# Stick-breaking attention in a hybrid trunk: weights summed by parts, with differences of neighbouring values

## The chip, the core and the metric

The kernel runs on one core of one Trainium2 chip. The metric is the device time of the whole program in microseconds (us). The core's engines are TensorE (PE; its weight loads are shown apart as PEld), VectorE (DVE), ScalarE (ACT), GpSimd (POOL) and SyncE (SP, which here issues nearly all DMAs). Each works through its own instructions in the order in which they were built, and waits at an instruction until what it needs is there.

## What is computed

The input is one sequence of 2048 tokens with 1024 features, float32. An even layer normalizes it, projects it to queries, keys and values of 8 heads of 128, to a gate, and to the input of a state-space mixer with a gate of its own, joins both branches and projects back; an odd layer is gated linear attention. The part that matters here is the attention of the even layer:

```python
z = jnp.einsum('bthd,bshd->bhts', qf[:, q0:kend], kf[:, :kend])
...
causal = s_idx < t_idx
log_beta = jax.nn.log_sigmoid(z)
log_one_minus = jnp.where(causal, log_beta - z, 0.0)
rest = lax.cumsum(log_one_minus, axis=3, reverse=True) - log_one_minus
w = jnp.where(causal, jnp.exp(log_beta + rest), 0.0)
outs.append(jnp.einsum('bhts,bshd->bthd', w, vf[:, :kend]))
```

A query t gives the key s the weight beta(t,s) times the product of 1 - beta(t,j) over all keys j between s and t. Its output is the sum of the weighted values.

Write p(t,s) for the product of 1 - beta(t,j) over all j from s to t - 1. Then beta(t,s) times the product behind it is p(t,s+1) - p(t,s), so the sum over keys can be written by parts: the value of the last key of the block, plus the sum over s of p(t,s) times (value of s - 1 less value of s), with zero for the value ahead of the first token.

## The kernel before, in words

Every matmul operand is split into a high and a low part (`split`, L310: a copy on ACT makes the high part, a subtraction on another engine the low one), and three products of the parts stand for one (`mm3`, L66). The program runs in stages: the gates' projections and the state-space branch first (to about 598 us of the profiled execution), then attention (598 to 1752 us), then the output projection and the odd layer.

`attention` (L668) loops over 8 heads; in a head over 4 macro tiles m of 512 tokens; in a macro tile over 4 token tiles of 128. For a token tile, ACT and POOL split the normalized input (`sh` L711, `sl` L712), PE makes query, key and value together in 24 matmuls of 384 columns (`pp`, L67 to L69), ACT squares the query and key and sums them (`qk` L719), POOL makes the two reciprocal roots (`qkms` L54, `qkrs` L56), DVE scales (`qn` L725), PE transposes (`tp` L728). The value is taken from PSUM by ACT (`vhi` L721) and DVE (`vlo` L722).

Then come two pairs of query blocks for the macro tile, each against the key chunks c = m, m - 1, ..., 0 of 512 keys. For each of the pair's two blocks: PE makes the scores (`z`), ACT takes sigmoid(-z) into `om` (L760) and sigmoid(z) into `be` (L762), DVE runs the product from the last key to the first (`pt`, L764, a scan that begins with the value that the chunk to the right left), POOL multiplies `be` by it (L768), PE transposes the result (`w`, L771), ACT and DVE split that (`th` L773, `tl` L774). With both blocks done PE multiplies by the values (`av`, L782), DVE applies the gate (`ot`, L785), and SP stores it (L786) and loads the next gate (`zs`, L739).

The order on each engine is made by the scheduler of the tile framework, which is asked to place instructions by its own timing model; by it the projections of a macro tile lie among the attention work of the one before, and the next head's weights (L660) are loaded toward the end of a head. There are two buffers for `sh` and `sl`, two PSUM banks for `z`, two for `w`, and three buffers for `be` and for `pt`.

Of the kernel before, what the change touches and what calls it, by code (L numbers as in the profile page):

```python
# [9 lines left out]
F32 = mybir.dt.float32  # L10
# [3 lines left out]
ALU = mybir.AluOpType  # L14
# [35 lines left out]
def rsqrt_mean(e, pool, ss, n, dim, tag):  # L50
    """1 / sqrt(ss / dim + EPS) for a [P, n] tile of sums of squares."""
# [8 lines left out]
def behind(e, i, first):  # L60
    """i comes behind first in their engine's queue"""
    e.tc.add_manual_dep(i.ins, first.ins.name, mybir.DependencyInfo(
        mybir.DependencyClass.NoSync, mybir.DependencyReason.DATA), reason="order")
# [8 lines left out]
class Norm:  # L72
    """hT[m][p, k, t] = rms_norm(x)[m * 512 + t, k * 128 + p], a token tile at a time"""
# [48 lines left out]
def s5_angles(e, s, lam_re, lam_im, log_dt):  # L122
    """lam, dt and sines of the angle of lam_bar and of its half; partitions and columns as in s5_setup"""
# [32 lines left out]
def s5_setup(e, room, lr, li, dt, sn, sh, b_re, b_im, c_re, c_im, dsk, bin_d, k0_d, co_d):  # L156
    """Chunk matrices of the SSM (8 tokens a chunk) into DRAM, powers of lam_bar into e.pw.

    Partition q = (parity, n) of pair i holds state n of group 2 * i + parity.
    bin_d[ri, i, (j, p), q] = lam_bar^(7-j) b_bar;  co_d[ri, i, q, (t, p)] = c lam_bar^(t+1)  # L160
    k0_d[g, (j, pi), (t, po)] = Re(c lam_bar^(t-j) b_bar) + d [t == j, pi == po]
    """
# [3 lines left out]
    # lam_bar^8, ^16, ^32, ^64: real parts, and (-im, im)  # L166
    e.pwr = [e.cst.tile([P, NI], F32, name=f"pwr{a}") for a in range(4)]
    e.pwi = [e.cst.tile([P, 2, NI], F32, name=f"pwi{a}") for a in range(4)]
    with e.pool("s5s", 1, "right") as s, e.pool("s5t", 2, "right") as s2, e.pool("s5w", 1, "right") as sw, \
# [41 lines left out]
        # powers  # L211
# [13 lines left out]
        def cmul(outs, xr, xi, yr, yi, sub, E):  # L225
            """outs[0] = xr yr + sub * xi yi, outs[1] = xr yi - sub * xi yr, x small, broadcast"""
# [24 lines left out]
        # G[tau] = c lam_bar^tau: real part, and minus the imaginary part  # L251
# [23 lines left out]
        # four groups at a time, on the partitions from 0, 32, 64 and 96  # L275
# [22 lines left out]
        # onto 16 partitions, then each row block of the chunk matrix  # L298
# [13 lines left out]
def split(nc, hi, lo, src, lo_eng):  # L312
    """hi + lo == src, each of 12 significant bits"""
# [7 lines left out]
# order in which a panel's last macro tile takes the weights: from low addresses on  # L321
# [3 lines left out]
class Panels:  # L325
    """Pools for weight panels of up to 512 columns, and for splits of hT."""
# [45 lines left out]
# token tiles to norm after these products (half, column block, row block)  # L372
# [3 lines left out]
def first_gates(e, pn, nrm, hT, w, c0, out_d, setup):  # L376
    """The first macro tile of gates(), as its tokens and weights come; returns the weights, and setup()."""
# [42 lines left out]
def gates(e, pn, hT, w, c0, out_d, row0, lo_eng, between=None, also=None, ws=None, sp=None, last=LAST):  # L420
    """out_d[row0 + f, t] = silu(h w[:, c0 + f]) for 512 columns; between(m) is called before macro tile m
# [925 lines left out]
```

## Time and profile before

| what | us |
|---|---|
| median of 3 runs | 2915.71 |
| lowest and highest run | 2911.27 and 2917.75 |
| span of the profiled execution | 2920.8 |
| of it, attention | 1154 |

The span runs from the first to the last instruction of the profiled execution. No separate time of that execution is given beside its span; the three runs are other executions. A row of the profile names line, engine, operation and tiles as out<-in; "busy" is the time in which an engine's instructions ran, and the idle time before an instruction is put down to what came last of the things that it waited for. Matmuls overlap one another, so the length of one in a row is longer than the step from one to the next.

### The profile page before, as it was taken

The page shows a single profiled execution, that of the slowest core. Times are in us where ns is not written, and L with a number is a line of the kernel's source. Part 1 is how long each engine was busy: PE and PEld are TensorE (multiplying, and loading weights), DVE is VectorE, ACT ScalarE, POOL GpSimd, SP SyncE. Part 2 cuts the span into 40 slices and gives each one's busy share as a digit, 9 for nine tenths or more (in the row PEclk, how much of TensorE's full clock was granted, in tenths as well). Part 3 has the DMA queues.
Part 4 walks back from the last instruction along what each step waited for, and adds up shares of the span by engine and source line. Part 5 has one row for each costly group of instructions (what it writes and reads, how often), then busy time and mean ns, then how long its engine had stood idle before and what let it go on. Part 6 is the DMA issues. An engine that isn't in the chain of part 4 may idle for free.

```text
span 2920.8 us, 46867 instructions
## 1 busy us (share of the span) xinstructions
PE 2795.6 (96%) x17433; PEld 2508.1 (86%) x17433; DVE 1766.5 (60%) x2789; ACT 1476.4 (51%) x3244; POOL 1446.3 (50%) x1513
## 2 busy tenths in 40 slices
PE   7989979899999999999999989999999999999999
PEld 6788767898989898989898978888788999999887
DVE  7768965757686767676767674223344556565521
ACT  5475224556666656665656663222345556555310
POOL 7102821478787878787878752000023465555300
PEclk9999989999999999999999999999999999999999
DMA  5532136411010101010102114333131111121343
GB/s 167 153 79 79 58 103 216 142 30 33 19 33 19 33 19 33 22 34 19 33 19 65 48 44 141 105 104 93 58 101 37 37 59 55 41 73 62 115 142 112
DMA packets 217011, 207.17 MB, mean 71 GB/s; under 512 B 24528, under 2 KB 185712, under 8 KB 216272
## 3 DMA queue, kind: packets, MB, share of 16 engines
q1 hardware_dynamic: 216208, 202.08, 22.5%
q8 instruction: 138, 2.26, 0.3%
q10 hardware_dynamic: 576, 2.10, 0.2%
q14 instruction: 89, 0.73, 0.1%
HBM read 129.29 MB, written 74.58 MB: 70 GB/s over the span
## 4 chain that ended last, share of the span: by engine, by line
PE 73%; DVE 8%; POOL 8%; issue 5%; ACT 3%; DMA 3%; SPq 1%; POOLq 0%; ACTq 0%; DVEq 0%
PE av L782 5%; PE pp L68 5%; PE pp L67 5%; PE ops L68 5%; PE pp L69 5%; PE ops L67 5%; PE ops L69 5%; PE gps L67 4%; PE gps L68 3%; PE gps L69 3%; PE w L771 3%; DVE pt L764 2%; PE qk L67 2%; PE qk L69 2%; PE qk L68 2%
## 5 line engine op out<-in xcount | busy, mean ns | idle before, releaser
L768 POOL TENSOR_TENSOR be<-be,pt 128x512 f32<-128x512 f32 (+2 forms) x320 | 359.1, 1128 | 162.5 <-DVE pt L764 87.5
L712 POOL TENSOR_TENSOR sl<-hT,sh 128x1024 fp32r<-128x1024 f32 x128 | 331.6, 2591 | 65.0 <-ACT sh L711 64.0
L68 PE MATMUL pp<-wlo,sh 128*128 128x384 f32 x1024 | 353.0, 345 | 8.0 <-POOL wlo L315 8.0
L67 PE MATMUL pp<-whi,sh 128*128 128x384 f32 x1024 | 356.8, 349 | 2.3 <-ACT whi L314 2.3
L69 PE MATMUL pp<-whi,sl 128*128 128x384 f32 x1024 | 348.4, 340 | 0.0
L764 DVE TENSOR_TENSOR_SCAN pt<-om,pt,zero 128x513 f32<-128x513 f32 x192 | 318.7, 1660 | 19.6 <-ACT om L760 12.5
L67 PE MATMUL gps<-sh,whi 128*128 128x512 f32 (+1 forms) x672 | 253.2, 390 | 24.0 <-DVE sg L365 20.7
L68 PE MATMUL gps<-sl,whi 128*128 128x512 f32 (+1 forms) x672 | 259.3, 387 | 3.4 <-DVE sl L315 3.3
L69 PE MATMUL gps<-sh,wlo 128*128 128x512 f32 (+1 forms) x672 | 257.0, 385 | 0.0
L773 ACT ACTIVATE th<-w 128x512 fp32r<-128x512 f32 (+2 forms) x320 | 171.9, 542 | 114.1 <-PE w L771 113.0
L774 DVE TENSOR_TENSOR tl<-w,th 128x512 fp32r<-128x512 f32 (+2 forms) x320 | 187.3, 597 | 66.2 <-ACT th L773 64.7
L760 ACT ACTIVATE om<-z 128x512 f32<-128x512 f32 (+2 forms) x320 | 174.5, 545 | 104.2 <-PE z L69 75.5
L68 PEld LDWEIGHTS pp<-wlo,sh 128*128 128x128 f32 x1024 | 193.7, 189 | 18.1 <-POOL wlo L315 15.6
L315 DVE TENSOR_TENSOR sl<-hT,sh 128x1024 fp32r<-128x1024 f32 (+1 forms) x148 | 173.0, 1192 | 51.0 <-ACT sh L314 49.0
L67 PEld LDWEIGHTS pp<-whi,sh 128*128 128x128 f32 x1024 | 195.0, 190 | 8.2 <-ACT whi L314 5.4
L69 PE MATMUL ops<-woh,ol 128*128 128x512 f32 x496 | 196.7, 397 | 0.0
L68 PE MATMUL ops<-wol,oh 128*128 128x512 f32 x496 | 196.3, 396 | 0.0
L67 PE MATMUL ops<-woh,oh 128*128 128x512 f32 x496 | 195.6, 395 | 0.0
L69 PEld LDWEIGHTS pp<-whi,sl 128*128 128x128 f32 x1024 | 193.0, 189 | 2.4
L314 ACT ACTIVATE sh<-hT 128x1024 fp32r<-128x1024 f32 (+1 forms) x148 | 155.6, 1090 | 61.6 <-PE gps L69 32.6
L711 ACT ACTIVATE sh<-hT 128x1024 fp32r<-128x1024 f32 x128 | 135.9, 1062 | 97.7 <-PE pp L68 97.1
L771 PE MATMUL w<-ident,be 128*128 128x128 f32 x1088 | 170.7, 274 | 8.5 <-POOL be L768 5.8
(326 smaller groups left out, 8249.2 us busy)
## 6 DMA issues: line engine op xcount, KB each, us to landing
zs_d<-sg SPq DMA_DIRECT2D x80, 256.0 KB
o<-o_d SPq DMA_DIRECT2D x80, 256.0 KB
xt<-in_x_dram SPq DMA_DIRECT2D x28, 512.0 KB
r<-in_even_w_in_dram SPq DMA_DIRECT2D x64, 192.0 KB
zs<-zs_d SPq DMA_DIRECT2D x64, 128.0 KB
o_d<-ot SPq DMA_DIRECT2D x64, 128.0 KB
r<-in_odd_w_in_dram SPq DMA_DIRECT2D x64, 128.0 KB
zs<-zs_d SPq DMA_DIRECT2D x32, 256.0 KB
```

Source lines behind the costliest of these rows:

```text
L67: nc.tensor.matmul(out, lhsT=lhi, rhs=rhi, start=start, stop=False)
L68: nc.tensor.matmul(out, lhsT=lhi, rhs=rlo, start=False, stop=False)
L69: return nc.tensor.matmul(out, lhsT=llo, rhs=rhi, start=False, stop=stop)
L314: a = nc.scalar.activation(hi, src, AF.Copy)
L315: b = lo_eng.tensor_tensor(lo, src, hi.bitcast(F32), ALU.subtract)
L712: nc.gpsimd.tensor_tensor(sl, ht, sh.bitcast(F32), ALU.subtract)
L760: nc.scalar.activation(o[:, lo:512], z[:, :n], AF.Sigmoid, scale=-scale)
L764: nc.vector.tensor_tensor_scan(pt[:, lo:][:, ::-1], o[:, lo:][:, ::-1], zr.to_broadcast([P, n + 1]), 1.0 if prev[i] is None else prev[i], ...
L768: nc.gpsimd.tensor_tensor(be[:, :n], be[:, :n], pt[:, lo + 1:513], ALU.mult)
L771: nc.tensor.transpose(w[:, s, :], be[:, s * P:(s + 1) * P], e.ident)
L773: nc.scalar.activation(th[:, :ni, qs], w[:, :ni, :], AF.Copy)
L774: nc.vector.tensor_tensor(tl[:, :ni, qs], w[:, :ni, :], th[:, :ni, qs].bitcast(F32), ALU.subtract)
```

## The change

The beta of a key and its product with the scan are gone. What is transposed is the scan itself, `pt`, and the values are replaced by differences of neighbouring values. The value goes from PSUM into `vf` (ACT, float32). Differences are made for two token tiles at a time (a half): DMAs move `vf` down by one partition into `dv` (rows 0 to 111 by one DMA, rows 112 to 126 by another, and for the first partition the last row of the tile before, by one DMA in the second half and one or two in the first), POOL subtracts, ACT and POOL split. The last value of each block of 128 is brought onto columns through DRAM (`ve_d`, `ve`) and added when the gate is applied, which is now two instructions instead of one. In the first half of a macro tile POOL's subtraction is held behind the `sl` of the last token tile. `pt` has four buffers instead of three.

```diff
         kvp = pool("at_kv", 5)
-        wk = pool("at_wk", 3)
+        vp = pool("at_v", 2)
+        wk = pool("at_wk", 4)
...
+                vf = vp.tile([P, 4, P], F32, tag="vf", name="vf")
                 for half in range(2):
...
-                        nc.gpsimd.tensor_tensor(sl, ht, sh.bitcast(F32), ALU.subtract)
+                        a = nc.gpsimd.tensor_tensor(sl, ht, sh.bitcast(F32), ALU.subtract)
+                        if i == 3:
+                            behind(e, sub, a)
...
-                        nc.scalar.activation(vhi[:, i, :], ps[:, 2, :], AF.Copy)
-                        nc.vector.tensor_tensor(vlo[:, i, :], ps[:, 2, :], vhi[:, i, :].bitcast(F32), ALU.subtract)
+                        nc.scalar.activation(vf[:, i, :], ps[:, 2, :], AF.Copy)
...
+                    i = slice(half * 2, half * 2 + 2)
+                    dv = vp.tile([P, 2, P], F32, tag="dv", name="dv")
+                    nc.sync.dma_start(out=dv[1:113], in_=vf[0:112, i])
+                    nc.sync.dma_start(out=dv[113:P], in_=vf[112:P - 1, i])
+                    if half:
+                        nc.sync.dma_start(out=dv[0:1], in_=vf[P - 1:P, 1:3])
+                    else:
+                        if m == 0:
+                            nc.vector.memset(dv[0:1, 0], 0.0)
+                        else:
+                            nc.sync.dma_start(out=dv[0:1, 0], in_=vl[P - 1:P, 3])
+                        nc.sync.dma_start(out=dv[0:1, 1], in_=vf[P - 1:P, 0])
+                    sub = nc.gpsimd.tensor_tensor(dv, dv, vf[:, i], ALU.subtract)
+                    split(nc, vhi[:, i], vlo[:, i], dv, nc.gpsimd)
+                    vl = vf
...
+                ve = vp.tile([P, 4], F32, tag="ve", name="ve")
+                nc.sync.dma_start(out=ve_d[h:h + 1, m * 4:m * 4 + 4], in_=vf[P - 1:P])
+                nc.sync.dma_start(out=ve, in_=ve_d[h, m * 4:m * 4 + 4].rearrange("i d -> d i"))
...
                             nc.scalar.activation(o[:, lo:512], z[:, :n], AF.Sigmoid, scale=-scale)
-                            be = wk.tile([P, 512], F32, tag="be", name="be")
-                            nc.scalar.activation(be[:, :n], z[:, :n], AF.Sigmoid, scale=scale)
                             pt = wk.tile([P, 513], F32, tag="pt", name="pt")
...
-                            nc.gpsimd.tensor_tensor(be[:, :n], be[:, :n], pt[:, lo + 1:513], ALU.mult)
                             w = wps.tile([P, 4, P], F32, tag="w", name="w")
                             for s in range(ni):
-                                nc.tensor.transpose(w[:, s, :], be[:, s * P:(s + 1) * P], e.ident)
+                                nc.tensor.transpose(w[:, s, :], pt[:, lo + s * P:lo + (s + 1) * P], e.ident)
...
-                    nc.vector.tensor_tensor(ot, av, zs, ALU.mult)
+                    for i in range(2):
+                        qs, b = slice(i * P, (i + 1) * P), pr % 2 * 2 + i
+                        nc.vector.scalar_tensor_tensor(ot[:, qs], av[:, qs], ve[:, b:b + 1], zs[:, qs], ALU.add, ALU.mult)
```

The scheduler orders the engines anew. Three places follow, all in the fifth head where the projections of the third macro tile (`hT2`) begin; numbers behind the names are buffer numbers and differ between the two programs.

First POOL before, from the split of the third macro tile's first token tile to a product in its third:

```order
L712 TENSOR_TENSOR sl_13761<-hT2_89,sh_13760 128x1024 [waits PE_49,Activation_49]
L54 TENSOR_SCALAR qkms_13498<-ss_13495 128x2 [waits Activation_49]
L56 TENSOR_TENSOR qkrs_13500<-qkms_13498,mhalf_68 128x2 [waits Pool_49]
L712 TENSOR_TENSOR sl_13805<-hT2_89,sh_13804 128x1024 [waits PE_49,Activation_49]
L54 TENSOR_SCALAR qkms_13542<-ss_13539 128x2 [waits Activation_49]
L768 TENSOR_TENSOR be_13568<-be_13568,pt_13570 128x128 [waits DVE_49,Activation_49]
L768 TENSOR_TENSOR be_13583<-be_13583,pt_13585 128x256 [waits DVE_49,Activation_49]
L56 TENSOR_TENSOR qkrs_13544<-qkms_13542,mhalf_68 128x2 [waits Pool_49]
L768 TENSOR_TENSOR be_13606<-be_13606,pt_13608 128x512 [waits DVE_49,Activation_49]
L712 TENSOR_TENSOR sl_13854<-hT2_89,sh_13853 128x1024 [waits PE_49,Activation_49]
L768 TENSOR_TENSOR be_13623<-be_13623,pt_13625 128x512 [waits DVE_49,Activation_49]
```

POOL after, from the same split on to that of the third token tile; `dv_13359` and `vlo_13169` are the second half of macro tile two:

```order
L719 TENSOR_TENSOR sl_13556<-hT2_89,sh_13555 128x1024 [waits PE_49,Activation_49]
L54 TENSOR_SCALAR qkms_13306<-ss_13303 128x2 [waits Activation_49]
L56 TENSOR_TENSOR qkrs_13308<-qkms_13306,mhalf_68 128x2 [waits DVE_49,Pool_49]
L719 TENSOR_TENSOR sl_13599<-hT2_89,sh_13598 128x1024 [waits PE_49,Activation_49]
L54 TENSOR_SCALAR qkms_13349<-ss_13346 128x2 [waits Activation_49]
L56 TENSOR_TENSOR qkrs_13351<-qkms_13349,mhalf_68 128x2 [waits DVE_49,Pool_49]
L750 TENSOR_TENSOR dv_13359<-dv_13359,vf_13172 128x256 [waits DMAHW5_49,DMAHW6_49,DMAHW0_49,Activation_49]
L315 TENSOR_TENSOR vlo_13169<-dv_13359,vhi_13168 128x256 [waits Activation_49]
L719 TENSOR_TENSOR sl_13655<-hT2_89,sh_13654 128x1024 [waits PE_49,Activation_49]
```

The products with beta are gone, and a subtraction and a low part for each half have come in, which stand behind the two reciprocal roots and ahead of the split of a token tile two further on.

Then ACT before, from the squares of the last token tile of the second macro tile (`pp_13513`) on:

```order
L719 ACTIVATE qk_13538,ss_13539<-pp_13513 128x128
L721 ACTIVATE vhi_13367<-pp_13513 128x128
L760 ACTIVATE om2_5874<-z_13562 128x128 [waits PE_49]
L762 ACTIVATE be_13568<-z_13562 128x128
L760 ACTIVATE om0_5872<-z_13577 128x256 [waits PE_49]
L762 ACTIVATE be_13583<-z_13577 128x256 [waits Pool_49]
L760 ACTIVATE om1_5873<-z_13601 128x512 [waits PE_49]
L762 ACTIVATE be_13606<-z_13601 128x512 [waits Pool_49]
```

ACT after, from the same squares on (`pp_13320`); `vhi_13168<-dv_13359` is the copy of the differences:

```order
L728 ACTIVATE qk_13345,ss_13346<-pp_13320 128x128 [waits PE_49,Activation_49]
L728 ACTIVATE qk_13345,ss_13346<-pp_13320 128x128
L730 ACTIVATE vf_13172<-pp_13320 128x128
L788 ACTIVATE om2_5875<-z_13378 128x128 [waits PE_49]
L788 ACTIVATE om0_5873<-z_13390 128x256 [waits PE_49]
L314 ACTIVATE vhi_13168<-dv_13359 128x256 [waits DMAHW5_49,DMAHW6_49,DMAHW0_49,Pool_49]
L788 ACTIVATE om1_5874<-z_13411 128x512 [waits PE_49]
L798 ACTIVATE th_13376<-w_13386 128x128 [waits PE_49]
L788 ACTIVATE om2_5875<-z_13425 128x512 [waits DVE_49,PE_49]
```

The second sigmoid of each score tile is gone; the copy of the value has become one to `vf`, and two sigmoids behind it stands the copy that waits for the DMAs and for POOL.

At last SP before, with a store and a gate load in turn:

```order
L786 DMA o_d_80<-ot_13022 128x256 [waits DVE_49]
L739 DMA zs_13311<-zs_d_79 128x256 [waits DMAHW6_49,DMAHW2_49]
L786 DMA o_d_80<-ot_13307 128x256 [waits DMAHW3_49,DVE_49]
L739 DMA zs_13558<-zs_d_79 128x256 [waits DMAHW4_49,DMAHW0_49]
L786 DMA o_d_80<-ot_13362 128x256 [waits DMAHW5_49,DVE_49]
L739 DMA zs_13651<-zs_d_79 128x256 [waits DMAHW2_49]
```

SP after, from the DMAs of the same second half on:

```order
L743 DMA dv_13359<-vf_13172 1x16x16 [waits DMAHW5_49,Activation_49,Pool_49]
L740 DMA dv_13359<-vf_13172 112x256 [waits DMAHW6_49,Activation_49]
L813 DMA o_d_80<-ot_13162 128x256 [waits DMAHW7_49,DVE_49]
L741 DMA dv_13359<-vf_13172 15x256 [waits DMAHW0_49]
L760 DMA ve_d_5864<-vf_13172 1x512 [waits DMAHW1_49]
L767 DMA zs_13456<-zs_d_79 128x256 [waits DMAHW2_49]
L748 DMA dv_13641<-vf_13172 1x16x8 [waits DMAHW3_49,Pool_49]
L761 DMA ve_13370<-ve_d_5864 128x4x1 [waits DMAHW4_49,DMAHW1_49]
L749 DMA dv_13641<-vf_13553 1x16x8 [waits DMAHW5_49,Activation_49]
```

Where SP had two DMAs for a pair of blocks, the pieces of `dv`, the store of the last values (`ve_d`) and their load (`ve`) have come in between; the store of a pair (`ot_13162`) stands between the two pieces of `dv_13359`.

## Rows read from the trace of the kernel before

**Rows 1.** The page's head and first part.

```profile
span 2920.8 us, 46867 instructions
...
PE 2795.6 (96%) x17433; PEld 2508.1 (86%) x17433; DVE 1766.5 (60%) x2789; ACT 1476.4 (51%) x3244; POOL 1446.3 (50%) x1513
```

**Rows 2.** Windows: us; busy of PE, PEld, DVE, ACT, POOL (count); granted clock; DMA share; GB/s.

```profile
598.00:1752.00 1154.00, 1118.57 (x7180) 1040.67 (x7180) 817.23 (x1219) 724.64 (x1907) 913.37 (x761) 1.00 0.10 31
1690.00:1752.00 62.00, 53.99 (x332) 46.63 (x333) 50.28 (x65) 38.68 (x80) 31.71 (x30) 0.97 0.17 50
1126.99:1269.72 142.73, 140.09 (x907) 130.65 (x906) 99.09 (x153) 90.58 (x240) 116.33 (x97) 1.00 0.09 27
```

**Rows 3.** Waits of PE, 598 to 1752 us: total us, times, longest.

```profile
PE tp L728 <- DVE qn L725: 10.8, 12, 3.3
PE pp L68 <- POOL wlo L315: 8.0, 10, 1.1
PE w L771 <- POOL be L768: 5.8, 16, 1.0
PE w L771 <- DVE tl L774: 2.4, 3, 1.0
...
PE pp L67 <- ACT whi L314: 2.3, 5, 0.6
PE av L782 <- ACT be L762: 1.5, 1, 1.5
```

**Rows 4.** Waits of all engines, same stretch.

```profile
DVE qn L725 <- POOL qkrs L56: 163.2, 106, 3.5
...
POOL be L768 <- DVE pt L764: 87.5, 97, 3.4
```

**Rows 5.** The page's fifth part: the multiply by beta, all shapes.

```profile
L768 POOL TENSOR_TENSOR be<-be,pt 128x512 f32<-128x512 f32 (+2 forms) x320 | 359.1, 1128 | 162.5 <-DVE pt L764 87.5
```

**Rows 6.** Groups by line and shape, 598 to 1752 us.

```profile
L762 ACT ACTIVATE be<-z 128x512 f32<-128x512 f32 x224 | 136.7, 610 | 0.0
...
L721 ACT ACTIVATE vhi<-pp 128x128 fp32r<-128x128 f32 x125 | 36.7, 294 | 0.0
L722 DVE TENSOR_TENSOR vlo<-pp,vhi 128x128 fp32r<-128x128 f32 x125 | 35.4, 283 | 28.5 <-ACT vhi L721 28.3
...
L785 DVE TENSOR_TENSOR ot<-av,zs 128x256 f32<-128x256 f32 x64 | 26.5, 415 | 30.9 <-PE av L782 30.8
...
L731 ACT ACTIVATE khi<-tp 128x256 fp32r<-128x256 f32 x63 | 24.3, 386 | 67.1 <-DVE qlo L732 67.0
...
L768 POOL TENSOR_TENSOR be<-be,pt 128x256 f32<-128x256 f32 x32 | 21.3, 667 | 6.5 <-ACT vhi L721 5.2 <-DVE pt L764 1.1 <-issue 0.2
```

**Rows 7.** Source line of the scan: ns min/median/max, first and last start.

```profile
L764 DVE TENSOR_TENSOR_SCAN pt<-om,pt,zero x192: 1260/1538/3393, 628.5 to 1742.6; 128x513 f32<-128x513 f32 x192
```

**Rows 8.** Source line of the gate's load: SP's own time for one issue.

```profile
L739 SPq DMA_DIRECT2D zs<-zs_d x64: 332/424/782, 586.7 to 1718.5; - x64
```

**Rows 9.** The chain of waits, whole run: start us, us, what.

```profile
155.78 2.02 DMA ka<-kt
...
522.28 6.43 DMA yk<-y_d
...
984.38 2.40 DMA r<-in_even_w_in_dram
```

**Rows 10.** Timeline of PE: start us, us.

```profile
1186.01 0.33 PE L68 MATMUL pp<-wlo,sh 128*128 128x384 f32 x1
1186.18 0.33 PE L69 MATMUL pp<-whi,sl 128*128 128x384 f32 x1
...
1187.63 0.28 PE L782 MATMUL av<-th,vlo 128*128 128x256 f32 x1
1187.75 0.28 PE L782 MATMUL av<-th,vhi 128*128 128x256 f32 x1
```

More of the change, by code (lines that the diff above doesn't have):

```diff
@@ L665, in load, with attention @@
         return out
-def attention(e, hT, w_in, zsT, oT, ap, w0, after):
+def attention(e, hT, w_in, zsT, oT, ve_d, ap, w0, after):
     nc, tc = e.nc, e.tc
@@ L1277, in after_head @@
             ow.early, ow.again = 6, (4, 5, 2, 3)
-    attention(e, hT, w0, zs_d, o_d, ap, aw, after_head)
+    attention(e, hT, w0, zs_d, o_d, dram("ve_d", [HEADS, NT, DH]), ap, aw, after_head)
     ow.pool("left")
```

## The prediction

> **What bounds the kernel now.** I read the page's head first, then windows, PE's waits, the waits of the other engines, and at last single rows for durations. PE is busy 96% of the span of 2920.8 us [rows 1]; no other engine is above 60%. The change touches attention alone, 598 to 1752 us. There PE is busy for 1118.57 of 1154 us at a granted clock of 1.00, so PE stands idle for 35.4 us, 3% of the stage [rows 2]. The work on PE is the same after the change: as many transposes, of `pt` instead of `be`, and the same three products. So the gain has a ceiling near 35 us, unless matmuls themselves run closer together, and the question is which part of those 35 us the change takes away and what new waits it brings.
>
> POOL is the second engine of the stage: 913.37 us, 79%; in one head it works for 116.33 of 142.73 us [rows 2]. PE's waits name what it is late with. Behind POOL directly: `pp` for `wlo`, 8.0 us, and `w` for `be`, 5.8 us. The largest, 10.8 us of `tp` for `qn`, names DVE [rows 3], but DVE itself waits for `qn` behind POOL's root `qkrs`, 163.2 us in 106 waits, 1.5 us each, for an instruction of two columns [rows 4]: the root stands in POOL's queue behind products with `be`. Products in turn wait for the scan `pt`, 87.5 us [rows 4], and hold up the splits and roots behind them. So 10.8 + 8.0 + 5.8 = 24.6 us of PE's waits end at POOL. The rest (`tl`, `whi`, `be` on ACT and smaller ones) has other causes [rows 3].
>
> **The change, part by part.**
>
> *The product with beta goes.* POOL loses 320 instructions, 359.1 us [rows 5], with the waits for `pt` ahead of them. All three causes above lose the work that stood in front.
>
> *The second sigmoid goes.* ACT loses 320 of them; the 224 wide ones took 610 ns each, 136.7 us [rows 6], the other 96 are narrower, so 137 to 137 + 96 x 0.61 = 195 us. PE waited for it once, 1.5 us [rows 3].
>
> *The differences come in on POOL and ACT.* For each of 64 halves POOL has a subtraction and a low part, 128x256 each, as the narrow product, 667 ns [rows 6]: 128 x 0.667 = 85.4 us. POOL's sum: 913.4 - 359.1 + 85.4 = 640 us, 55% of the stage. By the head that is 116.3 - 359.1 / 8 + 85.4 / 8 = 82 of 142.7 us, so a half (17.8 us) has 10.3 us of POOL work, and 7.5 us free. ACT: the copies of 128 columns stay (`vf` for `vhi`, 294 ns), and 64 copies of 128x256 come in at 386 ns, as `khi`: 25 us, far under what it loses. DVE loses 128 low parts, 36.2 us (283 ns each), and gains 64 `ot`: two of 128 columns cost between 2 x 0.283 and 2 x 0.415 for one of 0.415 [rows 6], so 10 to 27 us. None of the three is near its limit; I price them at nothing, under cover of PE's 96%.
>
> *The scan.* It takes 1538 ns at the median and 1260 ns at the least [rows 7]. What slows it isn't shown; if POOL's traffic beside it does, 192 scans x 0.28 us = 54 us come off DVE. DVE holds PE up for 2.4 us by `tl` [rows 3], so I count nothing for it.
>
> *The DMAs come in.* 280 more on SP. One issue holds SP for 424 ns at the median, 782 at most [rows 8]: 280 x 0.42 = 119 us of SP in 1154, under cover, as SP had 128 there. What matters is the chain from `vf` to the copy `vhi`, since ACT waits at that copy, and the sigmoids behind it feed the scans of the next blocks. POOL waits at the subtraction too, with a split and two roots behind it. The issue takes 0.42 us, and 0.4 more when a store of `ot` stands between two pieces, as in the change's listing. The landing of such a shift by one partition is not in this trace. The nearest row is `kt` to `ka`, SBUF to SBUF as here, at 2.02 us; a load of weights took 2.40, and `yk`, queued behind others, 6.43 [rows 9]. I take 2.02 as nearest in kind, with DMA at 10% here [rows 2], and keep 6.43 as the other end; below 2.02 nothing is gained, since no cover is needed then. With POOL's 0.67 the chain is 3.1 to 3.5 us.
>
> PE's work meanwhile, in the place listed (the end of a macro tile's projections): 10 `av` at 0.12 us, 17 `pp` at 0.17 [rows 10], two score blocks on the diagonal and a full one, estimated from `av`'s step by columns at 0.6 and 0.7 us, and two transposes, some 0.2. Together 5.6 us, of which ACT first uses 0.9 for two squares and the `vf` copy. That leaves 4.7 us against 3.1 to 3.5, and some of it goes into handing over between engines, so I reckon with a spare of about 1 us. In the first half of a macro tile there is more, since the subtraction there stands behind the split of the fourth token tile. The loss at 2.02 us is nothing. Where one piece lands late, or the next head's weights go ahead in the same queues, I allow 2 us in all.
>
> The Trainium skill speaks against this part: "DMA: Bandwidth & Descriptors", section "Rules for kernel authors", says that many small transfers are mostly fixed overhead, and gives about 2 us of that for each; 280 of them would be 560 us of transfer time by it, as an estimate, but they run beside each other and beside PE. The row of 2.02 us agrees with the figure; by either the sum stays as it is.
>
> *The last values* go to DRAM and back in two DMAs, at most 2 x 6.43 + 2 x 0.78 = 14.4 us [rows 8, 9], and are first needed at the first `ot` of the macro tile; the next macro tile's projections and a pair's blocks lie between, of 35.7 us for a macro tile (a quarter of a head). Price: nothing.
>
> **Sum.** 24.6 + 1.5 (`be` on ACT) - 2 = 24 us. Against the profiled execution: 2920.8 - 24 = 2896.8 us of span. That span is 5.1 us above the median of 2915.71, so the median comes to 2915.7 - 24, about 2892. If half of the 24 us stays as waits on the next link, 2904; if everything of the 35.4 us and a little of the scan's goes, 2878. That is this case's own range.
>
> **Rivals.**
>
> *The next link takes the waits.* DVE works 99.09 us in a head, 69% [rows 2], and `tp` waits for `qn` on DVE; scans of up to 3.4 us [rows 7] can stand ahead of `qn` as products did of the root. For it: `tl` and `qn` are DVE's. Against it: DVE's wait for the root is 1.5 us each time, which means that it is there early. Then only `wlo` or less is gained, and with the DMAs' 2 us and more taken back, some 3 us: 2913.
>
> *More than the idle time is won.* The ends of matmuls are modelled, and weight loads are busy for only 1040.67 of 1154 us [rows 2], 113 us less. The timeline holds steps of PE that are longer than the rows call waits; if POOL's releases cause a fifth of these 113 us beyond the 24, it is 24 + 21 = 45 us: 2871. The scan's speed-up would work the same way. The Trainium skill, "Perfetto Trace Analysis", section "Identifying the Most-Contended Engine", holds that matmul busy time is a poor measure and the share of weight loads a better one; this trace has 97% against 90%.
>
> *Slower: ACT and POOL held by the landings.* The point from which it decides is a landing more than about 1 us above 2.02. At the middle between 2.02 and 6.43 [rows 9], 4.2 us, each second half of a macro tile is late by 4.2 - 2.0 - 1.0 = 1.2 us; 32 of them make 38 us, against the gain of 24: +14, so 2930. For it: three or four DMAs of small rows must all land, and stores and gate loads stand between them in SP's queue. Against it: 0.10 share of DMA, and scores in two banks that let PE run ahead. At 6.43 us throughout it would be 32 x 3.4 = 109 us, or 3001, for which nothing speaks but the row itself.
>
> **How the numbers follow.** A measurement of this kernel can tell about 0.2%, 5.8 us. Forecast (2892, own range 2878 to 2904): 0.53. Next link (2913): 0.15. More than the idle time (2871): 0.12. Held by the landings (2930 and up): 0.20. Faster by over 0.2%, below 2909.9: the first, the third, and a fifth of the second, 0.68. Within 0.2%: 0.10, most of the second. Slower: 0.22, the last and a small rest of the second. The range leaves out the far end of the landings (0.13) and the far end of the greater gain (0.05): 2864 to 2924.
>
> **What would show it.** In the profile after: no `be` on ACT or POOL; POOL near 640 us in attention; PE's waits there near 10 us, none for `wlo` or `qn` above 2 us in sum; DVE's wait for the root well below 163 us; the pieces of `dv` landing in about 2 us; ACT's wait at `vhi` short and not followed by a wait of PE for `z` or `w`. I am wrong if PE waits for scans or `tl` in place of the root, if PE waits behind `vhi`, or if PE's busy time itself shrinks.

## The result, and the profile after

The changed kernel takes 2873.59 us (median of 4 runs, 2869.48 to 2875.68) against 2916.73 us of the kernel before, measured beside it (2911.27 to 2921.36): ratio 0.985, 95% interval 0.9836 to 0.9865. It is 43.1 us faster; 24 were forecast.

First the page's head and first part of the changed kernel, beside [rows 1]:

```profile
span 2870.8 us, 46525 instructions
...
PE 2765.3 (96%) x17433; PEld 2496.6 (87%) x17433; DVE 1719.9 (60%) x2733; ACT 1365.0 (48%) x2988; POOL 1197.6 (42%) x1321
```

The two profiled executions are 50.0 us apart, the medians 43.1. Windows of the odd layer, before and then after (us; busy of PE, PEld, DVE, ACT, POOL; granted clock; DMA share; GB/s), show why:

```profile
2215.40:2740.00 524.60, 514.34 (x4131) 497.78 (x4130) 309.08 (x632) 299.79 (x640) 263.03 (x314) 0.98 0.18 56
```

```profile
2173.20:2691.00 517.80, 509.22 (x4130) 492.62 (x4129) 309.54 (x633) 298.37 (x639) 261.03 (x314) 1.00 0.18 57
```

The same work took 6.8 us less there at a granted clock of 1.00 instead of 0.98, in a stage that the change doesn't touch. The rest is attention. Windows again, from the first scores to the last `av`, the kernel before (the first of [rows 2], with ends set in the same way) and the changed one:

```profile
598.70:1750.60 1151.90, 1116.46 (x7170) 1038.84 (x7170) 815.84 (x1217) 723.24 (x1905) 911.43 (x758) 1.00 0.10 31
```

```profile
603.40:1708.30 1104.90, 1090.70 (x7170) 1030.78 (x7170) 769.86 (x1162) 612.33 (x1648) 663.20 (x564) 1.00 0.14 39
```

It is 47 us shorter, and begins 4.7 us later (603.4 against 598.7), which makes 42. PE's idle time is 1104.9 - 1090.7 = 14.2 us in place of 35.4: 21.2 us are gone. But PE's busy time fell too, by 25.8 us at the same 7170 matmuls. PE's waits in the stage (total us, times, longest), beside [rows 3], and three of other engines:

```profile
PE w L796 <- DVE tl L799: 6.0, 5, 1.9
PE av L807 <- DVE tl L799: 2.9, 7, 0.9
PE w L796 <- DVE pt L790: 2.3, 4, 0.8
PE av L807 <- ACT th L798: 0.9, 2, 0.7
```

```profile
ACT vhi L314 <- POOL dv L750: 117.7, 48, 4.1
...
DVE pt L790 <- ACT om L788: 93.5, 71, 3.1
...
DVE qn L733 <- POOL qkrs L56: 78.0, 69, 3.3
```

No wait of PE for POOL is left, nor for `qn`. What is left ends mostly at DVE's low parts and scans. ACT waits 117.7 us for the subtraction. And a row that the prediction counted as nothing has moved, the scan's (ns min/median/max), beside [rows 7]:

```profile
L790 DVE TENSOR_TENSOR_SCAN pt<-om,pt,zero x192: 1252/1277/3355, 632.5 to 1698.0; 128x513 f32<-128x513 f32 x192
```

Its median fell from 1538 to 1277 ns. So there are two candidates for what POOL's products had cost: the queue on POOL (the prediction's), and something that they did to DVE.

### The profile page after: what moved, and what is told of

Same layout as the page of the kernel before. It is cut to its first block, busy times and chain, and to the rows that moved or that the text cites. A ratio compares the mean times of both kernels' runs of the same rounds, so it can differ in the third digit from the quotient of the medians.

```text
span 2870.8 us, 46525 instructions
## 1 busy us (share of the span) xinstructions
PE 2765.3 (96%) x17433; PEld 2496.6 (87%) x17433; DVE 1719.9 (60%) x2733; ACT 1365.0 (48%) x2988; POOL 1197.6 (42%) x1321
## 4 chain that ended last, share of the span: by engine, by line
PE 78%; DVE 7%; POOL 4%; issue 4%; ACT 3%; DMA 3%; SPq 1%; ACTq 0%; POOLq 0%; DVEq 0%
PE av L807 6%; PE pp L68 6%; PE pp L67 6%; PE pp L69 6%; PE ops L69 5%; PE ops L68 5%; PE ops L67 5%; PE w L796 4%; PE gps L67 3%; PE gps L68 3%; PE gps L69 3%; PE qk L67 2%; PE qk L69 2%; PE qk L68 2%; PE z L68 2%
## 5 line engine op out<-in xcount | busy, mean ns | idle before, releaser
L719 POOL TENSOR_TENSOR sl<-hT,sh 128x1024 fp32r<-128x1024 f32 x128 | 322.2, 2518 | 343.0 <-ACT sh L718 304.8
L790 DVE TENSOR_TENSOR_SCAN pt<-om,pt,zero 128x513 f32<-128x513 f32 x192 | 279.2, 1477 | 38.0 <-ACT om L788 37.3
L67 PE MATMUL gps<-sh,whi 128*128 128x512 f32 (+1 forms) x672 | 252.8, 389 | 23.1 <-DVE sg L365 20.3
L798 ACT ACTIVATE th<-w 128x512 fp32r<-128x512 f32 (+2 forms) x320 | 163.9, 535 | 149.3 <-PE w L796 148.8
L790 DVE TENSOR_TENSOR_SCAN pt<-om,zero 128x129 f32<-128x129 f32 (+3 forms) x128 | 158.8, 1262 | 56.8 <-ACT om L788 56.2
L788 ACT ACTIVATE om<-z 128x512 f32<-128x512 f32 (+2 forms) x320 | 167.0, 538 | 37.6 <-PE z L784 22.7
L796 PE MATMUL w<-ident,pt 128*128 128x128 f32 x1088 | 165.2, 273 | 8.6 <-DVE tl L799 6.0
```

The costliest lines, as they stand in the source:

```text
L67: nc.tensor.matmul(out, lhsT=lhi, rhs=rhi, start=start, stop=False)
L719: a = nc.gpsimd.tensor_tensor(sl, ht, sh.bitcast(F32), ALU.subtract)
L788: nc.scalar.activation(o[:, lo:512], z[:, :n], AF.Sigmoid, scale=-scale)
L790: nc.vector.tensor_tensor_scan(pt[:, lo:][:, ::-1], o[:, lo:][:, ::-1], zr.to_broadcast([P, n + 1]), 1.0 if prev[i] is None else prev[i], ...
L796: nc.tensor.transpose(w[:, s, :], pt[:, lo + s * P:lo + (s + 1) * P], e.ident)
L798: nc.scalar.activation(th[:, :ni, qs], w[:, :ni, :], AF.Copy)
```

## The experiments

Each kernel was built from the changed one or from the one before by the lines shown; the scheduler ordered the engines anew each time. The change in the heading is against the median of the changed kernel, or of the kernel before where that is named.

**Products back on POOL, on the path (+76.9 us).**

```diff
-        wk = pool("at_wk", 4)
+        wk = pool("at_wk", 3)
...
+                            be = wk.tile([P, 512], F32, tag="be", name="be")
+                            nc.gpsimd.tensor_tensor(be[:, :n], pt[:, lo:512], pt[:, lo + 1:513], ALU.mult)
...
-                                nc.tensor.transpose(w[:, s, :], pt[:, lo + s * P:lo + (s + 1) * P], e.ident)
+                                nc.tensor.transpose(w[:, s, :], be[:, s * P:(s + 1) * P], e.ident)
```

> The change with a product on POOL put back on the path: 320 products of the scan with itself shifted by one column, of the same shapes as before's, into a tile that is transposed in place of the scan, three buffers each as before (the output is then not the weights' sum). My theory, that PE waited for POOL's queue: POOL comes to about 665 + 359 = 1020 us in attention, PE's waits for roots, low parts and the product return, and the time goes back by at least the 43 us won, to 2915 or above, since POOL also keeps the differences. Rival, that the second sigmoid on ACT was what cost: it stays within 10 us of the change's 2873.6. Rival, that only the other order on PE helped: not told apart by this run alone, since the order moves again.

Measured: 2950.48 us (2948.37 to 2951.38). POOL works 1018 us in attention, and the waits are back:

```profile
PE tp L736 <- DVE qn L733: 22.9, 34, 2.3
PE av L809 <- DVE tl L801: 8.7, 12, 1.9
PE w L798 <- POOL be L795: 7.6, 17, 1.0
PE w L798 <- DVE tl L801: 4.9, 4, 1.4
PE pp L68 <- POOL wlo L315: 4.7, 8, 1.0
```

With the second sigmoid still gone, the products alone take back more than all that was won; POOL, which keeps the differences too, is more loaded than before (1018 us against 911). So the gain came from taking the products off POOL.

**Products on POOL that nobody reads (+88.1 us).** The same product into a tile with two buffers; the transposes read `pt` as in the change.

```diff
+        bp = pool("at_b", 2)
...
+                            be = bp.tile([P, 512], F32, tag="be", name="be")
+                            nc.gpsimd.tensor_tensor(be[:, :n], pt[:, lo:512], pt[:, lo + 1:513], ALU.mult)
```

> The change with the same 320 products on POOL, written to a tile that nobody reads: POOL's load is back, but no transpose waits for a product. My theory: the load in POOL's queue is what PE's waits for roots and low parts came from (18.8 of the 24.6 us by the waits of before), so about three quarters of what the run with the product on the path loses, at least 20 us over 2873.6, and scans back at a median near 1.54 us. Rival, that it was the step through POOL between scan and transpose: within 6 us of the change.

Measured: 2961.74 us (2949.71 to 2967.41; the profiled execution is 77.2 us longer than that of the change). The scan's median is 1530 ns. So the step through POOL between scan and transpose was not the point: the load is. Why it is not a little faster than the run before it stays open.

**The second sigmoid back, unread (-4.0 us).**

```diff
+        bp = pool("at_b", 2)
...
                             nc.scalar.activation(o[:, lo:512], z[:, :n], AF.Sigmoid, scale=-scale)
+                            be = bp.tile([P, 512], F32, tag="be", name="be")
+                            nc.scalar.activation(be[:, :n], z[:, :n], AF.Sigmoid, scale=scale)
```

> The change with the second sigmoid back on ACT, written to a tile that nobody reads: ACT back by 137 to 195 us to about 780 of 1106 us in attention. My theory: PE waited for it 1.5 us in all, so within 6 us of 2873.6. Rival, that ACT's relief brought the gain: at least 20 us slower, with PE waiting for th, whi or the scans behind ACT.

Measured: 2869.60 us (2868.48 to 2871.15), which is no slower, with ACT busy for 741 us of attention in place of 612. ACT's relief gave nothing.

**Values without differences (-8.2 us).**

```diff
-                        nc.scalar.activation(vf[:, i, :], ps[:, 2, :], AF.Copy)
+                        nc.scalar.activation(vhi[:, i, :], ps[:, 2, :], AF.Copy)
+                        nc.vector.tensor_tensor(vlo[:, i, :], ps[:, 2, :], vhi[:, i, :].bitcast(F32), ALU.subtract)
...
-                    nc.sync.dma_start(out=dv[1:113], in_=vf[0:112, i])
...
-                nc.sync.dma_start(out=ve, in_=ve_d[h, m * 4:m * 4 + 4].rearrange("i d -> d i"))
...
+                    nc.vector.tensor_tensor(ot, av, zs, ALU.mult)
```

> The change without the differences: values split as before (a copy on ACT, a low part on DVE for each token tile), no DMAs for them, no last values added, one instruction for the gate; the scan is still what is transposed (the output is then a sum with the wrong values). It prices the whole chain of the differences. My theory: the chain is covered but for the first head's start, where attention began 4.7 us later than before, so 3 to 10 us faster than 2873.6. Rival, that ACT's 118 us of waits at the copy of the differences reach PE: 15 us faster or more.

Measured: 2865.44 us (2863.49 to 2869.13). Attention begins at 598.0 us there, 5.4 us earlier than in the change, and is 4.2 us shorter. So the differences cost little in all, and ACT's 118 us of waits a few us at most. It is not the price of the waits alone, since the run also takes 112 us off POOL and puts 19 on DVE. Nor does it show that the price is paid at the start: the run with `vf` in other memory, below, begins earlier still and is no shorter.

**More work on DVE (+59.0 us).**

```diff
+        dx = c1.tile([P, P], F32, name="dx")
...
+                            nc.vector.tensor_tensor(dx, e.ident, e.ident, ALU.subtract)
                             w = wps.tile([P, 4, P], F32, tag="w", name="w")
```

> The change with one more DVE instruction of 128x128 ahead of each of the 320 transposes of a block, which nobody reads: at some 0.2 to 0.28 us each 64 to 90 us of DVE, more than its scans lost when POOL's products went (their median fell from 1538 to 1277 ns). Theory, that PE waited for what stands in POOL's queue: DVE has room (771 of 1106 us busy), so under 10 us slower than 2873.6. Rival, that POOL's traffic slowed DVE and DVE is what PE waited for: as much slower as the products on POOL made it, some 40 us or more.

Measured: 2932.64 us (2927.61 to 2933.57). But the instructions do not run ahead of the transposes. They wait for nothing, and all 320 came in the first fifth of attention, as their tile's row shows (ns min/median/max, first and last start):

```profile
L795 DVE TENSOR_TENSOR dx<-ident x320: 258/291/2449, 585.3 to 829.9; 128x128 f32<-128x128 f32 x160
```

Windows of that stretch and of the rest of attention, in the order of [rows 2]:

```profile
601.50:830.00 228.50, 191.10 (x1121) 174.05 (x1120) 221.72 (x466) 95.00 (x266) 107.72 (x97) 0.93 0.10 26
830.00:1764.70 934.70, 921.50 (x6049) 867.77 (x6050) 654.72 (x984) 518.47 (x1381) 552.77 (x468) 1.00 0.14 40
```

DVE is busy for 97% of the stretch, and PE stands idle for 37 us of it. The change does the same part, up to the same `av`, in 172 us, and the rest in 933: the loss lies wholly where DVE was full. So the run shows that PE waits for DVE when DVE is full. It puts neither expectation to the test, and says nothing on what DVE's time costs where scans and `tl` are spread over the stage.

**Roots on DVE, in the kernel before (+20.3 us against before).**

```diff
-    nc.gpsimd.tensor_scalar(ms, ss, 1.0 / dim, EPS, ALU.mult, ALU.add)
+    g = eng or nc.gpsimd
+    g.tensor_scalar(ms, ss, 1.0 / dim, EPS, ALU.mult, ALU.add)
...
+    else:
+        g.tensor_tensor(rs, ms, e.mhalf[:, :n], ALU.mult)
...
-                        rs = rsqrt_mean(e, sm, ss, 2, DH, "qk")
+                        rs = rsqrt_mean(e, sm, ss, 2, DH, "qk", nc.vector)
```

The two small instructions for the roots of query and key move from POOL to DVE; the root itself is left out, and a multiply stands for it.

> [...] POOL's products stay. Theory: PE's waits for qn, 10.8 us as named, ended at roots that stood in POOL's queue behind products; with them on DVE the wait of DVE for the root, 163 us, goes, and the kernel is 10 to 25 us faster than before's 2916.6, between 2892 and 2907. Rival, that roots are late whatever engine makes them (DVE's scans stand ahead of them there): within 6 us of before or slower.

Measured: 2936.56 us (2933.27 to 2939.39), slower, where the theory had 10 to 25 us faster. The rows of the two small instructions' tiles in this run (ns min/median/max):

```profile
L55 DVE TENSOR_SCALAR qkms<-ss x128: 134/790/2310, 529.5 to 1718.0; 128x2 f32<-128x2 f32 x128
L60 DVE TENSOR_TENSOR qkrs<-qkms,mhalf x128: 143/163/2325, 529.7 to 1718.9; 128x2 f32<-128x2 f32 x128
```

An instruction of two columns takes 0.14 us, or up to 2.3, about as long as POOL's split `sl` takes (2.4). DVE and POOL side by side show why. Timeline of the kernel before, DVE and then POOL (start us, us):

```profile
684.98 3.39 DVE L764 TENSOR_TENSOR_SCAN pt<-om,pt,zero 128x513 f32<-128x513 f32 x1
```

```profile
684.90 2.39 POOL L712 TENSOR_TENSOR sl<-hT,sh 128x1024 fp32r<-128x1024 f32 x1
687.37 0.99 POOL L54 TENSOR_SCALAR qkms<-ss 128x2 f32<-128x2 f32 x1
```

The scan began 0.08 us after `sl` and ended 1.08 us after `sl` did (687.29), less than the 1.26 that it takes alone. So it seems to have stood still until `sl` was about done. The next instruction on POOL, of two columns and otherwise 0.19 us long, ended at 688.36, with the scan (688.37): the hold works in both directions. Over the whole stage, by the start of each of the 192 wide scans and the end of the POOL instruction then running: in the kernel before 138 began while POOL worked (the expectation below has 136), and their time above 1.265 us follows the rest of POOL's instruction (correlation 0.98, the rest less 0.2 us); in the change it is 87. `tl` and `qn`, which have one operand in PSUM, are not held (`qn` 0.344 us at the median beside products, 0.343 with POOL idle). The Trainium skill, "SBUF — State Buffer", section "SBUF: two separate sides", says this: a DVE instruction with two inputs in SBUF and a GpSimd instruction that reads SBUF shut each other out for a whole instruction. The scan reads `om` and a column of zeros, both in SBUF. The traces agree with the hold, but not with its length: the scans ran on some 0.18 us before the recorded end of POOL's instruction, and POOL's power instruction of two columns held none (numbers in the last section).

**The zero of the scan in PSUM (three runs).** By these rows, a scan with one operand in SBUF should not be held. The zero went into a free column of `av`'s PSUM bank, which became one fixed tile.

```diff
-        zr = e.zero
...
+        avz = aps.tile([P, 512], F32, name="avz")
+        zr = avz[:, 511:512]
+        nc.vector.memset(zr, 0.0)
...
-                    av = aps.tile([P, 256], F32, tag="av", name="av")
+                    av = avz[:, 0:256]
```

In the kernel before:

> The kernel before, with the zero that the scan adds at each step read from a column of av's PSUM bank in place of SBUF; nothing else. In the traces so far a wide scan that begins while POOL works is longer by the rest of POOL's instruction (136 of 192 scans of before, 0.47 us each; 87 in the change); instructions of DVE with one operand in PSUM are not. New theory, that the holding of scans behind POOL is a large part of what the product on POOL cost: scans fall to about 1.3 us at the median and in the mean, and the kernel is 20 to 35 us faster than 2916.6 with POOL as loaded as ever. Old theory, that only the queue on POOL counts: within 6 us of before, PE's waits for qn and wlo as they were. A scan with an operand in PSUM could also take longer by itself; then the row says by how much.

In the change:

> The change with the zero of the scan in PSUM. 40 us of its 192 wide scans are still holds. New theory: they go, 5 to 15 us faster than 2873.6, and DVE's busy time in attention falls by 40 us or more. Old theory: within 5 us.

In the run with unread products:

> The change with the 320 products on POOL that nobody reads, and the zero of the scan in PSUM: the load of POOL's queue without the holding of scans. New theory in its strong form (holds are nearly all): back to within 15 us of 2873.6. Old theory (the queue alone): stays above 2945, as without the move of the zero. Both in part: between, and the split is read off: what it gives back of the 88 us is the holds' share.

Measured: 3453.82 us (3446.46 to 3461.45), 3111.04 (3107.05 to 3113.56) and 3111.11 (3104.12 to 3117.37). The first one's scan, and what DVE and PE wait for in it:

```profile
L766 DVE TENSOR_TENSOR_SCAN pt<-om,pt,avz x192: 1271/1281/1283, 634.5 to 2270.3; 128x513 f32<-128x513 f32 x192
```

```profile
PE w L773 <- POOL be L770: 252.3, 173, 3.0
...
DVE pt L766 <- PE avz L784: 236.5, 93, 5.8
```

As times these runs say nothing on either theory: scan and `av` now share a tile, each scan waits for matmuls that it has nothing to do with (237 us), and that new wait sets the pace. As rows they settle the hold: all 192 scans take 1271 to 1283 ns, where the longest took 3393, though 55 of them began while POOL worked at splits, products or the like.

**A POOL load that does not read (+34.3 us).** This one parts queue and hold without a new bank. The Trainium skill, the same page, section "Who interferes with whom", has it that a GpSimd instruction which only writes is not shut out.

```diff
+        be = pool("at_b", 1).tile([P, 1152], F32, name="be")
...
-                            nc.vector.tensor_tensor_scan(
+                            sc = nc.vector.tensor_tensor_scan(
...
+                            ms = nc.gpsimd.memset(be[:, :n * 9 // 4], 0.0)
+                            e.tc.add_manual_dep(ms.ins, sc.ins.name, mybir.DependencyInfo(
+                                mybir.DependencyClass.Sync, mybir.DependencyReason.DATA), reason="order")
```

> The change with 320 instructions on POOL that wait for the scan as the products did, but only write (a memset of 9/4 of the block's columns into a tile that nobody reads, by the rows of a memset of 128 columns, 205 ns, and of one column, 99 ns, about 1.04 us for a full block where a product took 1.09). A queue on POOL as long as in the run with unread products, 88 us slower than the change. If a scan is held only by instructions of POOL that read SBUF, scans stay near 1.28 us. Theory of the queue: at least 60 of the 88 us are back, PE's waits at qn behind the roots too. Theory of the holds: under 25 us slower. Between: the split is read off. If the memset holds scans as well, their rows say so, and the run tells nothing new on the split.

Measured: 2907.86 us (2903.00 to 2911.43, 8 runs; its profiled execution is 35.0 us longer than that of the change). DVE and then POOL in its timeline, and the scan's line:

```profile
636.45 1.28 DVE L791 TENSOR_TENSOR_SCAN pt<-om,pt,zero 128x513 f32<-128x513 f32 x1
```

```profile
636.28 1.06 POOL L795 MEMSET be<- 128x1152 f32 x1 [1.22 <-DVE pt L791]
```

```profile
L791 DVE TENSOR_TENSOR_SCAN pt<-om,pt,zero x192: 1253/1278/3096, 634.9 to 1730.0; 128x513 f32<-128x513 f32 x192
```

A scan beside a memset keeps its 1.28 us (47 begin so; on average 0.01 us longer, with 0.42 us of the memset to go), so the trace agrees. The queue is there: PE waits 10.7 us for `qn` and 7.1 for `wlo`, as before the change (10.8 and 8.0). It costs 34 us by the medians where the products cost 88, or 35 of 77 by the profiled executions: 39 to 45%, between the two theories. The memsets put 262 us on POOL (926 less 663) where the products put 364; scaled by that, an estimate, the queue's share would be 48 of 88 or 49 of 77, half or somewhat more. But the run is not free of holds. Its wide scans are busy for 299 us, 20 more than in the change (beside the products 315), because `sl` and `wlo` on POOL hold them for longer (50 us in sum against 33). So how much of the 34 us is the queue alone is not shown. What goes beyond goes with what only the products do: they hold scans (and are held), and keep `pt`'s buffers longer. How it splits between these two was not tried, nor was the fourth buffer of `pt` undone by itself.

**A second hop for the differences (+36.6 us).**

```diff
-                    nc.sync.dma_start(out=dv[1:113], in_=vf[0:112, i])
-                    nc.sync.dma_start(out=dv[113:P], in_=vf[112:P - 1, i])
+                    d0 = vp.tile([P, 2, P], F32, tag="d0", name="d0")
+                    nc.sync.dma_start(out=d0[0:112], in_=vf[0:112, i])
+                    nc.sync.dma_start(out=d0[112:P - 1], in_=vf[112:P - 1, i])
+                    nc.sync.dma_start(out=dv[1:113], in_=d0[0:112])
+                    nc.sync.dma_start(out=dv[113:P], in_=d0[112:P - 1])
```

> The change with each half's rows copied by two DMAs to a second tile at the same partitions first, and from there moved down by one: the chain from the value to the difference gets some 3.5 to 5 us longer (two more issues on SP and one more landing). It tests the rival of the prediction, that the landings decide, and how much spare the chain has. By the prediction's spare of about 1 us: 2.5 to 4 us late in each of 32 second halves, 80 to 130 us slower. If ACT's waits at the copy of the differences have much more cover than I worked out: under 20 us slower.

Measured: 2910.17 us (2905.74 to 2915.24, 10 runs), between the two. From the end of the `vf` copy to the end of the subtraction the change takes 4.8 us (first halves) and 4.1 (second) at the median; this run 6.7 and 6.4. So 1.9 to 2.3 us of delay, less than the 3.5 to 5 that were expected, cost 36.6 us, 1.1 us for each of 32 macro tiles. PE's waits say where:

```profile
PE w L799 <- DVE pt L793: 14.0, 22, 1.7
PE tp L736 <- DVE qn L733: 9.7, 14, 2.2
PE av L810 <- ACT th L801: 6.6, 8, 0.9
```

In 9 of the 22 waits of `w` for the scan, 8.6 of 14.0 us, ACT had just stood at `vhi`, so that the sigmoids behind it were late, and with them scans and `w`: the place that the prediction's rival named. In 7 more, 3.8 us, ACT had stood at the high part of the next head's weights, whose DMAs are issued on the same SP. The cover is real but short.

**Other memory for `vf` (-0.4 us).**

```diff
-        vp = pool("at_v", 2)
         io = pool("at_io", 2)
+        vp = pool("at_v", 2)
```

> The change with the pool of the values, differences and last values taken after the other pools of attention, so that it lies in other memory. In the change the first copy to vf waited 4.5 us for a store of the stage before, and attention's first scores began 4.7 us later than before. Theory: that wait was for the memory that vf reuses, so it goes, and the kernel is 3 to 6 us faster than 2873.6. Rival, that the start is late by the chain of DMAs itself: within 2 us.

Measured: 2873.24 us (2871.28 to 2876.52). ACT's wait in the change that this was to take away:

```profile
591.92 0.28 ACT L730 ACTIVATE vf<-pp 128x128 f32<-128x128 f32 x1 [4.49 <-DMA o_d<-sg]
```

It is gone, and the first scores come at 596.1 us, 7.3 earlier. But the last `av` comes only 3.8 us earlier, and the run is no shorter: the 3 to 6 us of the theory did not come. Where the rest went back is not settled.

The runs side by side; all but the median from the profiled executions, first scores to last `av`, us:

| run | median | attention | PE busy | PE idle | DVE busy | POOL busy |
|---|---|---|---|---|---|---|
| before | 2916.7 | 1151.9 | 1116.5 | 35.4 | 816 | 911 |
| the change | 2873.6 | 1104.9 | 1090.7 | 14.2 | 770 | 663 |
| products on the path | 2950.5 | 1179.8 | 1123.9 | 55.9 | 844 | 1018 |
| products unread | 2961.7 | 1182.4 | 1120.3 | 62.1 | 830 | 1028 |
| memsets on POOL | 2907.9 | 1134.6 | 1107.9 | 26.7 | 788 | 926 |
| more on DVE | 2932.6 | 1163.2 | 1112.6 | 50.6 | 876 | 660 |
| second hop | 2910.2 | 1140.2 | 1104.6 | 35.6 | 781 | 681 |
| second sigmoid | 2869.6 | 1095.4 | 1086.9 | 8.6 | 784 | 645 |
| no differences | 2865.4 | 1100.7 | 1093.1 | 7.6 | 789 | 551 |
| `vf` in other memory | 2873.2 | 1108.4 | 1096.1 | 12.3 | 769 | 664 |
| before, roots on DVE | 2936.6 | 1170.3 | 1118.5 | 51.8 | 1036 | 725 |

## Why the prediction was right, and where it was wrong

Sign and range were right; the size was not. 43.1 us lie outside the likeliest case's own range (12 to 38) and near the case to which I gave 0.12, more than the idle time; the range holds it only because it was drawn wide enough for that case.

*PE's waits behind POOL.* "24.6 us of PE's waits end at POOL": all of them went, and the run with products brought them back. Idle time as named fell by 21.2 us; the sum had 24. This step was right.

*The ceiling of 35 us.* It failed: the 24 us of waits that the sum took away were worth more than their names say, and the sign that I gave for being wrong came true, PE's busy time shrank (25.8 us). The time that PE loses at a wait is more than the idle time that the rows name, since the matmul ahead of the wait is drawn with an end that lies well behind the next one's usual start. In the kernel before:

```profile
1134.00 0.40 PE L68 MATMUL z<-klo,qhi 128*128 128x512 f32 x1
1134.23 0.39 PE L69 MATMUL z<-khi,qlo 128*128 128x512 f32 x1
1135.64 0.45 PE L68 MATMUL pp<-wlo,sh 128*128 128x384 f32 x1 [1.02 <-POOL wlo L315]
```

The step of such a `z` is 0.23 us; this one took 1.41. 1.18 us are lost, 1.02 named. A wait of less than 0.16 us there has no name at all. Counted over both traces, with a step called long when it is over 0.1 us above the usual one of the same two neighbours: before, PE lost about 57 us in 155 long steps, in the change 21 in 48, so 36 of the 47 us are there. At the steps that have a named wait it lost 46 and 18.5, which is 28 less where the names fell by 21. The usual steps of the two orders add up to the same within 1 us, so PE's new order by itself brought nothing. The other 11 us are steps that are longer by less than 0.1 us, and what shortened them is open.

There is no fixed rate by which named time is worth more. The change's 21.2 us went with 47, 2.2 for one. Against the change, 1 us of named idle time went with 1.6 us of attention (more on DVE, second hop, products unread), 1.7 (second sigmoid), 1.8 (products on the path) or 2.4 (memsets), but with 0.6 without the differences; with `vf` in other memory the two moved against each other, and for the roots on DVE, against the kernel before, it is 1.1. I had this as a rival, from the gap that weight loads leave, and gave it 0.12 (its 21 us, too, should be 22.6, a fifth of 113). That gap closed from 113 to 74 us. The Trainium skill, "Perfetto Trace Analysis", section "Identifying the Most-Contended Engine", which the prediction cites there, was the better guide to the room left: by the share of weight loads the stage went from 90% to 93%, where PE's busy share went from 97% to 99%.

*The scan.* "DVE holds PE up for 2.4 us, so I count nothing for it." Whether that failed is open. What slowed the scan is shown: POOL's instructions hold it, and it holds POOL's. Wide scans lost 40 us of busy time (groups by line in attention, before and after):

```profile
L764 DVE TENSOR_TENSOR_SCAN pt<-om,pt,zero 128x513 f32<-128x513 f32 x192 | 318.7, 1660 | 19.6 <-ACT om L760 12.5 <-POOL be L768 2.6
```

```profile
L790 DVE TENSOR_TENSOR_SCAN pt<-om,pt,zero 128x513 f32<-128x513 f32 x192 | 279.2, 1477 | 38.0 <-ACT om L788 37.3 <-PE w L796 0.2
```

What this gave PE is not shown. For a part in the 47 us speaks that products cost 88 us where memsets of a like queue cost 34. Against it speaks the run with the second sigmoid: its wide scans were busy for 298 us, 19 more than in the change, and it was no slower. The run with more on DVE can't price it, since its instructions filled one stretch. A late root on POOL and a late scan may both reach PE through `qn` and `tl`, so PE's list of waits does not part them.

*POOL, ACT and DVE.* POOL: 663.2 us against 640, since the subtraction takes 0.80 and the low part 1.01 us in the mean in place of 0.667. The second sigmoid was worth nothing, as forecast.

*The chain of DMAs.* Forecast 3.1 to 3.5 us to the end of the subtraction; measured 4.1 to 4.8. ACT's wait at `vhi`, forecast short, is 117.7 us in 48 waits, but none of PE's waits names it. SP's own time for an issue, 0.42 us in the forecast, was 0.53 and 0.85 (ns min/median/max), beside [rows 8]:

```profile
L740 SPq DMA_DIRECT2D dv<-vf x64: 522/529/1399, 592.9 to 1662.7; - x64
L741 SPq DMA_DIRECT2D dv<-vf x64: 817/845/1869, 593.6 to 1663.2; - x64
```

Still the price was small, as forecast: without the differences the kernel is 8.2 us faster. I had not seen that the first `vf` copy stands behind a store of the stage before, but taking that wait away gave nothing. The rival of late landings, priced at 38 us for 2.2 us of delay, came out at 36.6 for 1.9 to 2.3 in the run that made the delay. With the spare of 1 us, 1.9 to 2.3 late in 32 second halves make 29 to 42 us, so the spare was about right; the 80 to 130 us that I expected of that run came from a delay taken too long.

## What to carry to other kernels

A ceiling read from PE's named idle time is none: here 21.2 us of it went with 47 us of the stage, and in most other runs one went with 0.6 to 2.4. Work taken off GpSimd can also free VectorE where VectorE's instructions have two operands in SBUF: read the spread of such an instruction (1260 ns at the least, 3393 at the most) as time that it stood held, and see what runs on GpSimd beside it; what that is worth to TensorE is another question. Before an experiment's time is read, see from its rows where the added instructions ran: the ones that wait for nothing all came in one stretch. A chain of DMAs off the critical path may cost almost nothing and still have about a microsecond to spare: delay it once to know.

## What the runs showed of the hardware

A memset on GpSimd (1.06 us) does not hold a scan, nor does GpSimd's power instruction of two columns (21 scans of the run with products on the path began with 0.55 us of it to go, and were 0.02 us longer); products, splits and subtractions do, to about 0.2 us before their recorded end. On DVE it was not only instructions with two operands in SBUF that stood held: `qkms` there, with one, took up to 2310 ns in place of 134. A DMA of 15 rows held SP for 845 ns, one of 112 rows for 529, both with 256 floats in a row.
